# The opening of a hybrid SSD and gated-delta layer: order of the first loads, an early square-root table, and a gate tile ahead of the narrow projection

## The chip, the cores and the metric

One NeuronCore of a Trainium2 chip runs the whole program. The metric is the device time of one execution in microseconds, and a version's number is the median of three such runs.

## What is computed

One decoder layer over 1024 prompt tokens and 8 decode tokens (1032 columns in all), in float32. Only the beginning matters here: `h` is the RMS norm of the tokens, and `proj = h @ w_in` is cut into pieces, among them the narrow ones (32 step sizes `dt`, 8 `beta` and 8 `a` columns) and the merge gates (16 tiles of 128 columns).

```python
h = _rms_norm(x, norm_mix)
proj = jnp.einsum('bld,de->ble', h, w_in).astype(f32)
z, xbc, dt_raw, qkv, gate, b_raw, a_raw, mgate = _split(proj, IN_SIZES)
...
qkv, new_gdn_conv = _causal_conv(qkv, s_gdn_conv.astype(f32), gdn_conv_w.astype(f32), None)
...
dt = jax.nn.softplus(dt_raw + ssm_dt_bias.astype(f32))
...
beta = jax.nn.sigmoid(b_raw)
g = -jnp.exp(gdn_a_log.astype(f32)) * jax.nn.softplus(a_raw + gdn_dt_bias.astype(f32))
```

Behind this stand the two recurrent branches, their gated merge, a SwiGLU feed-forward, per-layer embeddings and a last norm. The change touches none of them.

## The kernel before, in words

**Dense products.** A weight tile of 1024 x 128 is loaded as one buffer `wraw` (two of them, L145 and L198) and split into a rounded part `wh` and a remainder `wl`, in two halves of four 128-row blocks each (`split_raw`, L132 to L141: the rounded part by a copy on ScalarE, L138, the remainder by a subtraction on VectorE, L139). `wh` and `wl` have three buffers each. `load_w` (L143) gives its load and its split a high priority. A product has three chunks of 344 tokens (`dense_units`, L149); a chunk takes 24 matmuls (eight blocks by three), goes into one of three PSUM banks `pd`, and is then copied out by its `evac`. Buffers and banks of one name are given out in program order.

**Who orders the work.** The tile framework has a planner: within the waits on data and buffers it arranges each engine's instructions by program order and priority, with costs of its own for every instruction. On the chip each engine then goes through its list in order. All the loads in this account are issued by SyncE's queue (SP).

**The opening (L196 to L236).** Nine token tiles `xt` (128 tokens by 1024; the ninth has 8) are asked for by SP. After the first come the five small gain loads (`gain_cols`, L114: they become columns by a transpose and a copy, L111 and L112); after the fourth come the three strided loads of the narrow columns into `wsm` (L215), which is the first `wraw` buffer and was cleared by GpSimd (L199). Then, for three parts of three tiles: a Square with a sum on ScalarE (L223), a root (L224), a reciprocal and a scaling on VectorE (L225, L226) give `xn`; per 128 channels three transposes on TensorE (L232) fill a PSUM tile (five are open at once), from which ScalarE takes the rounded `h` (L234) and VectorE the remainder (L235). A product's first chunk needs the first part alone, the second the first and second, the third the second and third.

**Behind it (L309 to L393).** The narrow product (L328) fills `x1` (48 x 1032) with ScalarE's copy-out at L326, which adds `bias`; that tile and its loads (L314, L315) lie where the opening's tiles lay. Then two gate tiles are multiplied (`fill(0, FILL[0])`, L329; `FILL[0]` is 2): `fill_units` (L290) loads a tile, multiplies it, copies it out by L296 and stores it. From the whole of `x1` a row of steps on VectorE and ScalarE computes the step sizes and their cumulative sums (L331 to L361), which are transposed into `colA`, `colB` and `colQ` (L389, L390).

**After that.** The first gated-delta head begins: `proj` (L413) multiplies a tile, copies it to `raw` (L421; two buffers), and a convolution of four steps on VectorE (L433, L435) reads `raw` and the column tile `h_g`, which is made of six loads `cst` through one buffer, with four transposes each (L407, L410, L411). The PSUM tiles of these transposes follow those of L389.

Of the kernel before, what the change touches and what calls it, by code (L numbers as in the profile page):

```python
# [8 lines left out]
F32 = mybir.dt.float32  # L9
F32R = mybir.dt.float32r  # L10
AF = mybir.ActivationFunctionType
# [5 lines left out]
P = 128  # L17
# [16 lines left out]
FILL = (2, 6, 9, 12, 15, 17, 20, 22, 24)  # L34
# [5 lines left out]
def hybrid_step(  # L40
# [9 lines left out]
    V, S, G, TE = nc.vector, nc.scalar, nc.gpsimd, nc.tensor  # L50
# [5 lines left out]
    cp = ctx.enter_context(tc.tile_pool(name="cp", bufs=1, reuse_waits="tile"))  # L56
# [36 lines left out]
    def bias_col(v, name):  # L93
        t = cp.tile([P, 1], F32, name=name)
        G.memset(t, v)
        return t

    b_eps = bias_col(EPS, "b_eps")
    b_epsq = bias_col(128.0 * EPS, "b_epsq")

    gcols = cp.tile([P, 41], F32, name="gcols")
    cwm = cp.tile([P, 120], F32, name="cwm")
# [3 lines left out]
    def gain(base, k):  # L106
        return gcols[:, base + k : base + k + 1]
# [6 lines left out]
    def gain_cols(pool):  # L114
        r0 = pool.tile([41, P], F32, name="r0")
        for src, o, n in ((norm_mix, 0, 8), (norm_ffn, 8, 8), (norm_pl, 16, 8), (ssm_norm, 24, 16), (gdn_norm, 40, 1)):
            dma(r0[o : o + n, :], src[0].rearrange("(k p) -> k p", p=P))
        to_cols(r0, gcols, 41)

    def conv_cols(pool):  # L120
        r1 = pool.tile([120, P], F32, name="r1")
        for j in range(4):
            dma(r1[24 * j : 24 * j + 24, :], ssm_conv_w[0][j].rearrange("(k p) -> k p", p=P))
        dma(r1[96:120, :], ssm_conv_b[0].rearrange("(k p) -> k p", p=P))
        r2 = pool.tile([96, P], F32, name="r2")
        for j in range(4):
            dma(r2[24 * j : 24 * j + 24, :], gdn_conv_w[0][j].rearrange("(k p) -> k p", p=P))
        to_cols(r1, cwm, 120)
        to_cols(r2, cwg, 96)


    def split_raw(raw, nk):  # L132
        parts = []
        for k0 in range(0, nk, 4):
            n = min(4, nk - k0)
            wh = wp.tile([P, 4, P], F32R, name="wh", bufs=3)
            wl = wp.tile([P, 4, P], F32R, name="wl", bufs=3)
            S.copy(wh[:, :n], raw[:, k0 : k0 + n])  # L138
            V.tensor_tensor(wl[:, :n], raw[:, k0 : k0 + n], wh[:, :n].bitcast(F32), ALU.subtract)  # L139
            parts += [(wh[:, k], wl[:, k]) for k in range(n)]  # L140
        return parts  # L141
# [7 lines left out]
    def dense_units(wt, acts, evac, chunks=CHUNKS):  # L149

        n = len(acts)
        for t0, tn in chunks:
            ps = pd.tile([P, 512], F32, name="pd")
            o = ps[:, :tn]
            for i, (ah, al) in enumerate(acts):
                wh, wl = wt[i]
                h = ah[:, t0 : t0 + tn]
                mm(o, wh, h, i == 0, False)
                mm(o, wh, al[:, t0 : t0 + tn], False, False)
                mm(o, wl, h, False, i == n - 1)  # L160
            evac(t0, tn, o)
            yield

    def dense(wt, acts, evac, chunks=CHUNKS):
        for _ in dense_units(wt, acts, evac, chunks):
            pass
# [34 lines left out]
    with (  # L201
        tc.tile_pool(name="p0", bufs=1, side="right", reuse_waits="tile") as p0,
        tc.tile_pool(name="p0x", bufs=4, side="right", reuse_waits="tile") as p0x,
    ):
        xts = []
        for tt in range(9):
            n = P if tt < 8 else NB
            xt = p0x.tile([P, D], F32, name="xt", bufs=9)
            dma(xt[:n], x_prompt[0, tt * P : tt * P + P, :] if tt < 8 else x_sample[:, 0, :])
            xts.append(xt)  # L210
            if tt == 0:
                gain_cols(p0)
            if tt == 3:
                for o, c0, m in ((0, COL_DT, 32), (R_B, COL_BETA, 8), (R_A, COL_A, 8)):
                    dma(wsm[:, :, o : o + m], w_in[:, c0 : c0 + m].rearrange("(k p) f -> p k f", p=P))  # L215
        for g in range(3):
            t0, tn = PARTS[g]
            xns = []
            for tt in range(3 * g, 3 * g + 3):
                n, xt = (P if tt < 8 else NB), xts[tt]  # L220
                xn = p0x.tile([P, D], F32, name="xn", bufs=6)
                ss = p0x.tile([P, 1], F32, name="ss", bufs=9)
                S.activation(xn[:n], xt[:n], AF.Square, accum_out=ss[:n])  # L223
                S.activation(ss[:n], ss[:n], AF.Sqrt, bias=b_eps[:n], scale=1.0 / D)  # L224
                V.reciprocal(ss[:n], ss[:n])  # L225
                V.tensor_scalar(xn[:n], xt[:n], ss[:n], None, ALU.mult)  # L226
                xns.append((xn, n))
            for k in range(KD):
                pool, name = ((pt, "pt"), (py, "py"), (pz, "pz"), (pt, "pt"), (py, "py"))[k % 5]
                t = pool.tile([P, 512], F32, name=name)  # L230
                for j, (xn, n) in enumerate(xns):
                    TE.transpose(t[:, j * P : j * P + n], xn[:n, k * P : k * P + P], ident[:n, :n])  # L232
                h, l = (a[:, t0 : t0 + tn] for a in hacts[k])
                S.activation(h, t[:, :tn], AF.Copy, scale=gain(G_MIX, k))  # L234
                V.scalar_tensor_tensor(l, t[:, :tn], gain(G_MIX, k), h.bitcast(F32), ALU.mult, ALU.subtract)  # L235
        conv_cols(p0)  # L236
# [53 lines left out]
    def fill_units(lo, hi):  # L290

        for j in range(lo, hi):
            col, dst = (COL_M + j * P, sg_d[j]) if j < 16 else (COL_G + (j - 16) * P, gate_d[j - 16])
            t = mgp.tile([P, NT], F32, name="mg")
            wt = load_w(w_in[:, col : col + P], 8)
            for i, _ in enumerate(dense_units(wt, hacts, lambda t0, tn, o: S.copy(t[:, t0 : t0 + tn], o))):  # L296
                if i == 2:
                    dma(dst, t)
                yield

    def fill(lo, hi):
        for _ in fill_units(lo, hi):
            pass
# [5 lines left out]
    with tc.tile_pool(name="pr", bufs=1, side="right", reuse_waits="tile") as pr:  # L309
# [15 lines left out]
        def ev(t0, tn, o):  # L325
            S.activation(x1[:, t0 : t0 + tn], o[:NR], AF.Identity, bias=bias)  # L326

        dense(split_raw(wsm, 8), hacts, ev)  # L328
        fill(0, FILL[0])  # L329
        beta = pr.tile([NR, NT], F32, name="beta")  # L330
        S.activation(beta[R_B : R_B + 8], x1[R_B : R_B + 8], AF.Sigmoid)  # L331
        ta = pr.tile([NR, NT], F32, name="ta")
# [1007 lines left out]
```

## Time and profile before

| | us |
|---|---|
| median of 3 runs (lowest, highest) | 2725.28 (2723.42, 2728.84) |
| the profiled execution, its own time | 2733.16 |
| its span, first to last instruction | 2731.4 |
| granted TensorE clock, mean | 0.985 |

The profiled execution is 7.9 us (0.3%) longer than the median, and 1.8 us of its time lie outside its span. TensorE is the engine that is busy nearly throughout, so the table is read with one question: in which stretches does it have nothing to do, or run at the lower clock, and what ended each of them.

### The profile page before, as it was taken

The numbers are of one execution on the slowest core, as the hardware profiler recorded it, in microseconds if no ns is written. First come the engines' busy times: TensorE is split into PE (matmuls) and PEld (weight loads), VectorE is DVE, ScalarE is ACT, GpSimd is POOL, SyncE is SP. The second block draws the span as 40 slices with busy tenths as digits, with TensorE's granted clock in tenths as the row PEclk, the third lists the DMA queues.
The fourth block names the chain that finished last, engine by engine and source line by source line (L and its number), as shares of the span: only waits on it lengthen the run. The fifth ranks groups of instructions, "written<-read, shape, count | busy, mean of one in ns | idle before, by whom it ended". The sixth has DMA issues, their size and how long they took to land.

```text
span 2731.4 us, 43746 instructions
## 1 busy us (share of the span) xinstructions
PE 2635.8 (96%) x17431; PEld 2552.8 (93%) x17431; DVE 1554.0 (57%) x2757; ACT 1013.5 (37%) x2070; POOL 241.0 (9%) x493
## 2 busy tenths in 40 slices
PE   7999999689999999999999999999999999999998
PEld 7999989689989989898999989999999999999998
DVE  6677895866657567564455566534343333333465
ACT  5455644256346364343332235422212121212243
POOL 0101120030020120110010000011000000000020
PEclk9999999899999999999999999999999999999999
DMA  3345443365355363458674347411111111111132
GB/s 122 120 149 176 143 154 102 97 135 142 102 113 152 94 149 108 106 147 228 188 216 139 114 142 257 153 48 41 47 48 44 52 42 53 41 54 40 47 88 93
DMA packets 456665, 306.34 MB, mean 112 GB/s; under 512 B 44049, under 2 KB 430010, under 8 KB 455438
## 3 DMA queue, kind: packets, MB, share of 16 engines
q1 hardware_dynamic: 454062, 295.13, 37.5%
q10 hardware_dynamic: 2400, 8.42, 0.8%
q8 instruction: 137, 2.24, 0.3%
q14 instruction: 66, 0.54, 0.1%
HBM read 227.17 MB, written 76.31 MB: 111 GB/s over the span
## 4 chain that ended last, share of the span: by engine, by line
PE 81%; DMA 6%; DVE 5%; ACT 3%; issue 2%; POOL 1%; SPq 0%; DVEq 0%; POOLq 0%; ACTq 0%
PE pd L69 72%; PE py L69 4%; DMA ab<-acum_d 2%; PE pt L69 2%; PE pz L69 1%; DMA out_dram<-so 1%; ACT ab L694 1%; DVE stmp L567 1%; DVE ca L435 1%; POOL Xt L746 1%; DVE wl L139 0%; DMA wraw<-in_w_pl_gate_dram 0%; ACT wh L138 0%; DMA mg<-y_d 0%; DMA xt<-in_x_prompt_dram 0%
## 5 line engine op out<-in xcount | busy, mean ns | idle before, releaser
L69 PE MATMUL pd<-h,wh 128*128 128x344 f32 x6384 | 1543.6, 324 | 13.8 <-ACT zt L455 9.0
L69 PEld LDWEIGHTS pd<-h,wh 128*128 128x128 f32 x6384 | 1109.9, 189 | 24.9 <-ACT zt L455 9.9
L69 PE MATMUL pd<-h,wl 128*128 128x344 f32 x3192 | 1031.2, 323 | 0.5
L69 PEld LDWEIGHTS pd<-h,wl 128*128 128x128 f32 x3192 | 604.2, 189 | 4.2 <-DVE wl L139 2.4
L138 ACT CAST wh<-wraw 128x512 fp32r<-128x512 f32 (+1 forms) x386 | 234.5, 610 | 844.7 <-PE pd L69 826.3
L139 DVE TENSOR_TENSOR wl<-wraw,wh 128x512 fp32r<-128x512 f32 (+1 forms) x386 | 263.5, 684 | 328.1 <-ACT wh L138 324.5
L69 PE MATMUL pd<-gu,wh 128*128 128x344 f32 (+2 forms) x1056 | 249.1, 320 | 0.0
L69 PE MATMUL pd<-y,wh 128*128 128x344 f32 x768 | 187.5, 325 | 0.0
L69 PEld LDWEIGHTS pd<-gu,wh 128*128 128x128 f32 x1056 | 182.3, 188 | 0.1
L69 PE MATMUL pd<-gu,wl 128*128 128x344 f32 (+2 forms) x528 | 168.9, 320 | 0.0
L694 ACT ACTIVATE ab<-ab,ncolA 128x128 f32<-128x128 f32 x256 | 81.3, 391 | 147.9 <-POOL ab L690 147.6
L69 PEld LDWEIGHTS pd<-y,wh 128*128 128x128 f32 x768 | 133.4, 190 | 1.2 <-issue 0.2
L421 ACT COPY raw<-pd 128x344 f32<-128x344 f32 x144 | 63.1, 440 | 180.6 <-PE pd L69 172.5
L69 PE MATMUL pd<-y,wl 128*128 128x344 f32 x384 | 125.4, 327 | 0.0
L1229 DVE TENSOR_TENSOR acc<-acc,pd 128x344 f32<-128x344 f32 x120 | 61.3, 512 | 103.9 <-PE pd L69 103.5
L1208 DVE TENSOR_TENSOR lt<-rb,pd 128x344 f32<-128x344 f32 x66 | 33.9, 513 | 141.4 <-PE pd L69 141.4
L1164 POOL TENSOR_TENSOR sqs<-sqs,sqt 128x1032 f32<-128x1032 f32 x12 | 30.5, 2539 | 924.1 <-ACT sqt L1163 924.1
L69 PEld LDWEIGHTS pd<-gu,wl 128*128 128x128 f32 x528 | 99.2, 188 | 0.0
L69 PE MATMUL pd<-h,gw 128*128 128x384 f32 (+1 forms) x576 | 95.9, 326 | 1.8 <-DVE pg L1259 1.8
L435 DVE SCALAR_TENSOR_TENSOR ca<-raw,cwg,ca 128x1056 f32<-128x1056 f32 x72 | 96.3, 1338 | 0.8
L435 DVE SCALAR_TENSOR_TENSOR ca<-raw,cwm,ca 128x1056 f32<-128x1056 f32 x72 | 94.6, 1315 | 1.8
L69 PEld LDWEIGHTS pd<-h,gw 128*128 128x128 f32 x576 | 92.7, 191 | 2.8 <-DVE pg L1259 2.2
(389 smaller groups left out, 3448.0 us busy)
## 6 DMA issues: line engine op xcount, KB each, us to landing
wraw<-in_w_in_dram SPq DMA_DIRECT2D x88, 512.0 KB
wraw<-in_w_ffn_in_dram SPq DMA_DIRECT2D x44, 512.0 KB
ab<-acum_d SPq DMA_DIRECT2D x32, 512.0 KB
out_dram<-sd SPq DMA_DIRECT2D x48, 256.0 KB
wraw<-in_w_ffn_out_dram SPq DMA_DIRECT2D x40, 256.0 KB
sg_d<-mg SPq DMA_DIRECT2D x16, 516.0 KB
bb<-rk_d SPq DMA_DIRECT2D x8, 1024.0 KB
sd<-in_state_ssm_dram SPq DMA_DIRECT2D x32, 256.0 KB
```

The source lines that it names most:

```text
L69: TE.matmul(o, l, r, start=start, stop=stop)
L138: S.copy(wh[:, :n], raw[:, k0 : k0 + n])
L139: V.tensor_tensor(wl[:, :n], raw[:, k0 : k0 + n], wh[:, :n].bitcast(F32), ALU.subtract)
L421: S.copy(raw[:, 3 + t0 : 3 + t0 + n], o[:, :n])
L435: V.scalar_tensor_tensor(ca, raw[:, j : j + CONVN], w[j], ca, ALU.mult, ALU.add)
L567: V.tensor_tensor(tmp[:, :i, :i], xs[:, :i, :i], bc(blk[:, :i, i], 1, [P, i, i]), ALU.mult)
L694: S.activation(ab[:, h], ab[:, h], AF.Exp, bias=ncolA[:, c, h0 + h : h0 + h + 1])
L746: G.tensor_tensor(X[i][:, cs], X[i][:, cs], eb[:, i], ALU.add)
L1164: G.tensor_tensor(sqs[:, ts], sqs[:, ts], sq[:, :tn], ALU.add)
L1208: V.tensor_tensor(dst[:, t0 : t0 + tn], rb[:, t0 : t0 + tn], o, ALU.mult)
L1229: V.tensor_tensor(a, a, o, ALU.add)
```

## The change

Four edits. A one-column activation with a square root is issued as soon as its bias column is there. The gain loads come after the third token tile and not after the first. The narrow columns' loads come after the ninth token tile and not after the fourth. The first of the two gate tiles is multiplied ahead of the narrow product.

```diff
@@ -97,6 +97,8 @@
     b_eps = bias_col(EPS, "b_eps")
     b_epsq = bias_col(128.0 * EPS, "b_epsq")
+    warm = cp.tile([P, 1], F32, name="warm")
+    S.activation(warm, b_eps, AF.Sqrt)
@@ -208,9 +210,9 @@
             xts.append(xt)
-            if tt == 0:
+            if tt == 2:
                 gain_cols(p0)
-            if tt == 3:
+            if tt == 8:
                 for o, c0, m in ((0, COL_DT, 32), (R_B, COL_BETA, 8), (R_A, COL_A, 8)):
                     dma(wsm[:, :, o : o + m], w_in[:, c0 : c0 + m].rearrange("(k p) f -> p k f", p=P))
@@ -325,8 +327,9 @@
+        fill(0, 1)
         dense(split_raw(wsm, 8), hacts, ev)
-        fill(0, FILL[0])
+        fill(1, FILL[0])
         beta = pr.tile([NR, NT], F32, name="beta")
```

## Rows read from the trace of the kernel before

**Rows 1.** The page: busy time of each engine, share of the span, instructions.

```profile
PE 2635.8 (96%) x17431; PEld 2552.8 (93%) x17431; DVE 1554.0 (57%) x2757; ACT 1013.5 (37%) x2070; POOL 241.0 (9%) x493
```

**Rows 2.** Stretches: length, busy time by engine, granted clock, DMA share, GB/s.

```profile
0.00:5.00 5.00, 0.00 (x0) 0.00 (x0) 1.42 (x3) 1.99 (x2) 2.00 (x14) 1.00 0.51 169
5.00:10.00 5.00, 0.30 (x1) 0.18 (x1) 0.39 (x3) 3.43 (x8) 0.00 (x0) 1.00 0.92 310
10.00:15.00 5.00, 3.74 (x17) 3.20 (x18) 3.33 (x7) 3.87 (x9) 0.00 (x0) 1.00 1.02 228
15.00:20.00 5.00, 3.20 (x14) 2.10 (x13) 5.00 (x11) 5.00 (x12) 0.00 (x0) 0.79 0.75 287
20.00:25.00 5.00, 5.00 (x23) 4.87 (x22) 3.46 (x8) 3.75 (x10) 0.13 (x2) 0.53 0.46 125
...
40.00:45.00 5.00, 4.01 (x25) 3.74 (x24) 2.06 (x3) 4.79 (x8) 0.00 (x0) 1.00 0.38 105
```

**Rows 3.** Timeline of SP's queue: start, duration, line, target and source.

```profile
0.82 0.39 SPq L209 DMA_DIRECT2D xt<-in_x_prompt_dram  x1
...
3.00 1.62 SPq L209 DMA_DIRECT2D xt<-in_x_prompt_dram  x3
4.66 0.43 SPq L146 DMA_DIRECT2D wraw<-in_w_in_dram  x1
5.21 6.17 SPq L215 DMA_DIRECT2D wraw<-in_w_in_dram  x3
11.43 2.01 SPq L209 DMA_DIRECT2D xt<-in_x_prompt_dram  x4
```

**Rows 4.** Timeline of ScalarE, with the idle time before and its releaser.

```profile
4.30 1.06 ACT L223 ACTIVATE xn<-xt 128x1024 f32<-128x1024 f32 x1 [2.20 <-DMA xt<-in_x_prompt_dram]
...
6.99 1.06 ACT L223 ACTIVATE xn<-xt 128x1024 f32<-128x1024 f32 x1 [1.54 <-DMA xt<-in_x_prompt_dram]
7.95 0.19 ACT L223 ACTIVATION_READ_ACCUMULATOR xn<-xt 128x1 f32 x1
8.15 1.28 ACT L224 ACT_TABLE_LOAD   x1
...
11.00 0.29 ACT L224 ACTIVATE ss<-ss,b_eps 128x1 f32<-128x1 f32 x1
...
13.44 0.58 ACT L234 ACTIVATE h<-pt,gcols 128x384 fp32r<-128x384 f32 x1 [1.10 <-PE pt L232]
...
17.35 0.66 ACT L138 CAST wh<-wraw 128x512 fp32r<-128x512 f32 x1
```

**Rows 5.** Timeline of VectorE and TensorE around the first dense matmul.

```profile
11.70 0.75 DVE L226 TENSOR_SCALAR xn<-xt,ss 128x1024 f32<-128x1024 f32 x1
...
18.06 0.94 PE L69 MATMUL pd<-h,wh 128*128 128x344 f32 x2 [1.74 <-ACT wh L138]
```

**Rows 6.** The chain that ended last: start, us, what.

```profile
11.26 0.21 PE py L232
...
24.89 0.11 PE pz L232
...
41.27 34.33 PE pd L69 x216
```

**Rows 7.** Timelines of VectorE and ScalarE from the narrow result to the first convolution.

```profile
43.63 1.23 DVE L335 SCALAR_TENSOR_TENSOR ta<-x 48x1032 f32<-48x1032 f32 x1 [0.29 <-ACT x L326]
...
92.46 0.79 DVE L433 TENSOR_SCALAR ca<-raw,cwg 128x1056 f32<-128x1056 f32 x1 [0.34 <-POOL raw L417]
...
95.12 2.67 DVE L435 SCALAR_TENSOR_TENSOR ca<-raw,cwg,ca 128x1056 f32<-128x1056 f32 x2
...
100.81 0.44 ACT L421 COPY raw<-pd 128x344 f32<-128x344 f32 x1
```

**Rows 8.** TensorE's dense matmuls alone in one stretch, and its timeline there.

```profile
93.15:106.45 13.30, 11.61 (x71) 10.78 (x70) 0.00 (x0) 1.40 (x4) 1.00 0.46 149
...
106.50 0.48 PE L69 MATMUL pd<-h,wh 128*128 128x344 f32 x2
```

## The prediction

> **What bounds the kernel now.** I read the busy times first. TensorE is busy for 96% of the span [rows 1], so a change pays where TensorE has nothing to do, or runs at the lower clock, and where nothing behind takes the gain back. The stretches [rows 2] show where that is in the opening: TensorE is idle for 5.0, 4.7, 1.3 and 1.8 us in the first four stretches of 5 us, and for 1.0 us in the stretch from 40 to 45. From 15 to 25 the granted clock is 0.79 and 0.53 of 2.4 GHz, which is the level of 1.2 GHz for part of the time; the lost share is (0.21 + 0.47) x 5 = 3.4 us. TensorE had been idle for 1.74 us just before its first dense matmul at 18.06 [rows 5].
>
> What ended that idle time is in the queue and on ScalarE. SP asks for the first token tile at 0.82 and for the next three only from 3.00, behind the five gain loads; then come the first gate tile's weights (4.66) and the three narrow loads, which hold the queue for 6.17 us, so that the fifth token tile is asked for at 11.43 [rows 3]. ScalarE waits 2.20 us for the first tile and 1.54 us for the second, and loads a second function table (1.28 us) between the second Square and the first root [rows 4]. The first `h` is written at 13.44.
>
> Next I looked behind the opening for what waits on the narrow product. `x1` is whole when L335 begins, at 43.63; VectorE's chain for the step sizes follows, and the first convolution can begin only at 92.46, runs until 97.79 and so frees its `raw` buffer; the copy-out of the third projection's first chunk, which writes that buffer, ends at 101.25 [rows 7]. That projection fills all three PSUM banks. TensorE went through 71 recorded dense matmuls, one projection of 72, from 93.15 to 106.45, and began the next one, which needs the first bank again, at 106.50 [rows 8]. So this bank is free 5.25 us before it is wanted.
>
> **The change, part by part.** The sum is made against the profiled execution (2733.16 us, of which 2731.4 are span); a difference found there is taken off the median of 2725.28. A measurement of this kernel can tell about 0.2%, 5.5 us, from no change.
>
> *Token tiles first.* Three tiles back to back, then the gains, the fourth tile and, as I read the queue, the gate weights again in tenth place. In the stretch from 5 to 10 the transfers moved 310 GB/s at a busy share of 0.92 [rows 2]; at 310/0.92 = 337 GB/s a tile of 512 KB takes 1.6 us. With the first at 4.3 as before, the others land at about 5.9, 7.5 and 9.1 and the gate weights at 10.7. The third Square, at 9.84 before, begins at 7.5 and takes 1.15 us with its read (as the second, 6.99 to 8.14 [rows 4]); before, the third tile's root began at 11.00 and its scaled tile was ready at 12.45 [rows 4, 5], so now at 10.2, and the first `h` could be written at about 10.7 or 11.1. The gain loads, five issues that move behind two tiles, land at about 6, under the Squares; if they came after 10.7 each 1 us would cost 1 us of the first `h`.
>
> *Table at once.* The load of 1.28 us goes away between the Squares; an activation of one column comes in before the first tile has landed, where ScalarE waits 2.20 us anyway [rows 4]. If that cover were gone it would cost one load and one root, 1.6 us. Most of the 1.28 us lies under the wait for the second and third tile; I count nothing beside the times above. The Trainium skill, "ScalarE: Activation LUTs", section "What ACT_TABLE_LOAD costs", adds a drain to each switch, about 2.66 us in all. The trace does not agree: the root starts right behind the 1.28 us. By the page's figure the opening would give 1.4 us more, as an estimate.
>
> *Gate tile in front.* Its weights have the highest priority and are there at 10.7; ScalarE's two casts (0.66 each [rows 4]) then stand before the eight copies of `h`, which start at 12.0 and not at 10.7. The first dense matmul follows the first `h` (0.58) at 12.6, against 18.06 [rows 5], 5.4 us earlier. Less is transposed by then (18 transposes and not 24, at 0.11 us [rows 6]), 0.6 us of work that is still to be done: 4.8 us gained. Bounds: if the casts fall behind the copies of `h`, 2 us less; if ScalarE has the first `h` at 10.7 and the casts just after it, 1.3 us more.
>
> *The stall at 40 to 45 goes.* It is the wait for the narrow copy-out, whose bias is loaded late; now a gate tile's chunks come first and are copied out without a bias: 1.0 us gained, 0 at worst.
>
> *Between the parts.* One chunk of the gate tile, one half of the narrow product's and the transposes are all that TensorE can do until the second part's `h` is there. I take 1.0 us lost, with bounds 0 and 3. The lower clock I take to cost as much as before, 3.4 us, with bounds 0 and 5.
>
> *Narrow loads last.* Their 6.17 us of issues no longer stand before five token tiles. Behind them in the queue are now only the second gate tile's weights and the convolution columns, which wait for buffers anyway. The narrow weights, at about 20 us, are covered by the gate tile's first chunk and the transposes; if that cover fails the loss is in the 1.0 above.
>
> So the gate tile and the narrow product, which end at 41.27 + 72 x 34.33/216 = 52.7 now [rows 6], end at 52.7 - (4.8 + 1.0 - 1.0) = 47.9. **That is 4.8 us gained at this point** (bounds -1 and 10).
>
> *What is late next.* The narrow product now ends last of the two. With its copy-out (some 0.5 us) and the start of L335, `x1` is whole at 48.6 and not at 43.63: 5.0 us later. Everything on the path to the first convolution hangs on it, VectorE's chain, the transposes and, behind them, the `cst` loads. The bank that was free at 101.25 is free at 106.25, or 105.65 where the copy-out, which then has ScalarE to itself, comes 0.6 sooner. TensorE, 4.8 us ahead, wants it at 101.7, and waits 4.0 us; it can do nothing else, since all three banks are held. It goes on at 105.65 instead of 106.50. The sum of both shifts is fixed: each microsecond more in the opening makes the narrow result less late, and the net gain is the opening's gain less 4.0 (bounds 3 and 5.5). **Net: 0.8 us.** 2733.16 becomes 2732.4, and the median 2724.5.
>
> **The rivals.** *The opening's gain is kept.* If the narrow product's chunks are done before the gate tile's last one, or the chain behind `x1` has more room than I find, the bank is never late. For it: in the stretch from 40 to 45 VectorE is busy for 2.06 of 5 us [rows 2]. Against it: the second half of the narrow weights needs a `wh` buffer which the gate tile gives back only in its last chunk, and the 5.25 us of room are less than the two shifts together (9.8). It gives 4.8 to 10 us, with 7 as the middle: 2718. Chance 0.25.
>
> *ScalarE stands behind the gate weights.* Its list is fixed beforehand. If the planner puts the two casts ahead of the third Square, ScalarE waits at that place until the weights land. This decides when they land after 7.5, and I expect 10.7. The Square is then at 12.0, the first `h` at some 15.2 and the first dense matmul at 15.8; the later parts move as well, the opening gains 2.3 us less the starving of up to 3, about -1, and with the 4.0 to 5.5 of the late narrow result the kernel loses 5 to 6.5: 2731. For it: the casts have the highest priority; against it: the weights follow the fourth tile in the queue. Chance 0.15.
>
> *The lower clock stays away.* The clock fell after TensorE had stood idle and came back only while dense matmuls ran [rows 2, 5]. If dense work follows the first transposes closely enough the 3.4 us are saved, and the net gain is 4.2: 2721. If the gaps between transposes are longer, as three tiles that land one by one may make them, up to 1.6 us more are lost. Chance 0.08. The Trainium skill, "TensorE: Matmul & The Clock Gate", section "What's actually happening", has the lower level as the default and the higher as what sustained work releases; the trace agrees with the order, and by that rule the earlier dense work would bring the clock back earlier.
>
> *The change does not do what it says*, since the first gate tile's weights were asked for early before as well and the rest is moved about under TensorE's later work. That is within the forecast's own range.
>
> **How the numbers follow.** The forecast, a gain in the opening that the late narrow result takes back, has 0.52, with a range of its own from 2720 to 2729 (the bounds of its terms, rarely all at one end). Kept gain 0.25, ScalarE's wait 0.15, clock 0.08. The range goes from 2716, the middle of the kept gain and some more, to 2731: about 0.1 is left out on each side. Faster by over 0.2% is below 2719.8: most of the kept gain and a little of the others, 0.27. Slower by over 0.2% is above 2730.7: 0.14, from ScalarE's wait and the tail of the forecast. The rest, 0.59, is within.
>
> **What would show it.** In the changed profile the third Square should begin near 7.5 with no table load before the roots, the casts of the gate tile near 10.7 and the first dense matmul near 12.6; both products should be done near 48. L335 should start near 48.6, and TensorE should show an idle time of some 4 us just before 106, released by a copy-out to `raw`. If that wait is not there, the kept gain is right and I am wrong by its size; if ScalarE waits for weights ahead of the third Square, the slower rival holds.

## The result, and the profile after

| | before | after |
|---|---|---|
| median, us (lowest, highest; six runs each) | 2724.76 (2722.35, 2729.67) | 2739.03 (2733.98, 2744.08) |
| profiled execution, its own time | 2733.16 | 2739.25 |
| its span | 2731.4 | 2737.5 |
| granted TensorE clock, mean | 0.985 | 0.986 |

The ratio of the means of these runs is 1.0048 (95% interval 1.0033 to 1.0063): the change makes the kernel 0.48% slower. The medians lie 14.3 us apart, and "the 14 us" below are these. The busy time of TensorE is the same as before [rows 1]:

```profile
PE 2634.1 (96%) x17431; PEld 2550.6 (93%) x17431; DVE 1552.4 (57%) x2757; ACT 1013.1 (37%) x2071; POOL 245.7 (9%) x493
```

As a ruler I use the start of the n-th recorded matmul into a `pd` bank, counted from 0 (14192 are recorded in either kernel). The 264th begins 1.8 us earlier in the changed kernel, the 384th 0.3 us earlier, the 432nd 5.0 us later and the 456th 8.6 us later (119.4 and 110.8). So the opening gained a little, and between 95 and 120 us much more was lost. The stretches show where (length; busy time and number of instructions of TensorE, its weight loads, VectorE, ScalarE and GpSimd; granted clock, DMA share, GB/s); they answer to [rows 2]:

```profile
10.00:15.00 5.00, 3.62 (x16) 3.02 (x17) 3.38 (x9) 3.14 (x9) 0.00 (x0) 1.00 0.74 284
15.00:20.00 5.00, 5.00 (x28) 4.93 (x29) 4.96 (x11) 4.68 (x11) 0.00 (x0) 1.00 0.50 122
20.00:25.00 5.00, 3.56 (x24) 2.60 (x23) 3.04 (x7) 5.00 (x13) 0.13 (x2) 1.00 0.69 147
...
30.00:35.00 5.00, 4.13 (x28) 3.21 (x26) 4.09 (x11) 3.03 (x8) 0.00 (x0) 0.94 0.01 3
...
40.00:45.00 5.00, 5.00 (x33) 5.00 (x33) 0.84 (x2) 3.00 (x5) 0.00 (x0) 1.00 0.66 211
...
85.00:90.00 5.00, 5.00 (x16) 4.00 (x17) 2.28 (x6) 1.53 (x2) 0.00 (x0) 0.56 0.73 194
90.00:95.00 5.00, 5.00 (x30) 3.83 (x28) 2.43 (x7) 1.64 (x5) 0.18 (x1) 0.76 0.10 33
...
105.00:110.00 5.00, 1.38 (x11) 1.05 (x9) 4.93 (x5) 2.04 (x3) 0.13 (x1) 0.95 0.80 227
110.00:115.00 5.00, 3.23 (x16) 2.75 (x17) 2.63 (x4) 2.63 (x8) 1.62 (x4) 0.50 0.33 125
115.00:120.00 5.00, 5.00 (x30) 5.00 (x29) 4.31 (x6) 2.14 (x4) 0.24 (x2) 0.87 0.17 64
```

From 15 to 20 and from 40 to 45 TensorE is busy throughout, where it was idle for 1.80 and 0.99 us before. But it is idle for 1.44 us from 20 to 25 and for 0.87 us from 30 to 35 (0 and 0.10 us before). From 105 to 115 it is idle for 5.39 us, and before and behind that it runs in part at 1.2 GHz: idle time and lost clock, (1 - granted clock) x busy time, come to 0.1 + 3.4 us from 80 to 105 and 5.4 + 2.3 us from 105 to 130. The kernel before shows neither between 50 and 130 us; two of its stretches:

```profile
105.00:110.00 5.00, 5.00 (x34) 5.00 (x33) 3.78 (x6) 4.06 (x8) 0.73 (x3) 1.00 0.57 168
110.00:115.00 5.00, 5.00 (x33) 5.00 (x33) 4.42 (x7) 2.86 (x7) 0.20 (x1) 1.00 0.12 45
```

The granted clock of 1.00 that the first stretches show is not borne out by the matmuls: the first two dense ones, at 15.39, took 0.92 us together, about as long as the two at 18.06 before [rows 5] and twice the 0.48 us of the two at 106.50 [rows 8]; before, a transposition took 0.21 us at 11.26 and 0.11 at 24.89 [rows 6]. So in either kernel the loss to the lower clock in the opening is larger than these rows give.

The opening first. SP's queue (start, duration, line, target and source), beside [rows 3]:

```profile
4.33 0.36 SPq L211 DMA_DIRECT2D xt<-in_x_prompt_dram  x1
...
7.43 1.57 SPq L211 DMA_DIRECT2D xt<-in_x_prompt_dram  x3
16.54 0.38 SPq L148 DMA_DIRECT2D wraw<-in_w_in_dram  x1
16.96 0.58 SPq L211 DMA_DIRECT2D xt<-in_x_prompt_dram  x1
...
18.01 3.99 SPq L217 DMA_DIRECT2D wraw<-in_w_in_dram  x3
```

The weights of the second gate tile stand ahead of the last token tiles and of the narrow loads, and wait for a buffer: the queue issues nothing from 9.00 to 16.54. ScalarE, beside [rows 4]:

```profile
7.43 1.06 ACT L225 ACTIVATE xn<-xt 128x1024 f32<-128x1024 f32 x1 [0.71 <-DMA xt<-in_x_prompt_dram]
...
8.60 1.28 ACT L101 ACT_TABLE_LOAD   x1
9.90 0.20 ACT L101 ACTIVATE warm<-b_eps 128x1 f32<-128x1 f32 x1
10.01 0.65 ACT L226 ACTIVATE ss<-ss,b_eps 128x1 f32<-128x1 f32 x3
...
13.55 0.58 ACT L236 ACTIVATE h<-pt,gcols 128x384 fp32r<-128x384 f32 x1 [1.86 <-PE pt L234]
...
14.49 1.14 ACT L140 CAST wh<-wraw 128x512 fp32r<-128x512 f32 x2
```

The third Square is 2.4 us earlier than before, and the first `h` is not (13.44 before). The planner put `warm` behind the third Square, so the table load is still there, and all three roots stand behind it.

From the narrow result to the first convolution (copy-out of the last narrow chunk, start of the chain, last transposed column, first convolution, the activation that reads its result, the copy-outs of the third projection), beside [rows 7]:

```profile
51.45 0.54 ACT L328 ACTIVATE x<-pd,rbias 48x344 f32<-48x344 f32 x1
52.19 1.22 DVE L338 SCALAR_TENSOR_TENSOR ta<-x 48x1032 f32<-48x1032 f32 x1
95.24 0.36 DVE L393 COPY colQ<-pt 128x192 f32<-128x192 f32 x1 [0.56 <-PE pt L392]
104.90 0.79 DVE L436 TENSOR_SCALAR ca<-raw,cwg 128x1056 f32<-128x1056 f32 x1
110.26 1.06 ACT L439 ACTIVATE kq<-ca 128x1024 f32<-128x1024 f32 x1 [2.30 <-DVE ca L438]
...
111.45 1.12 ACT L424 COPY raw<-pd 128x344 f32<-128x344 f32 x3
```

`x1` is whole 8.6 us later than before, and the first convolution begins 12.4 us later. TensorE's own waits, beside [rows 5, 8]:

```profile
15.39 0.92 PE L69 MATMUL pd<-h,wh 128*128 128x344 f32 x2
22.39 0.33 PE L234 MATMUL pt<-ident,xn 128*128 128x128 f32 x1 [0.88 <-DVE xn L228]
110.45 0.59 PE L413 MATMUL pt<-ident,cst 24*128 24x24 f32 x4 [4.08 <-DMA cst<-in_state_gdn_conv_dram]
111.94 0.65 PE L69 MATMUL pd<-h,wh 128*128 128x344 f32 x1 [0.90 <-ACT raw L424]
113.02 0.59 PE L413 MATMUL pt<-ident,cst 24*128 24x24 f32 x4 [0.42 <-DMA cst<-in_state_gdn_conv_dram]
```

And the queue just before that wait:

```profile
95.59 0.31 SPq L410 DMA_DIRECT2D cst<-in_state_gdn_conv_dram  x1
...
104.34 0.33 SPq L525 DMA_DIRECT2D gb<-acum_d  x1
104.83 0.38 SPq L148 DMA_DIRECT2D wraw<-in_w_in_dram  x1
106.41 4.98 SPq L410 DMA_DIRECT2D cst<-in_state_gdn_conv_dram  x2
```

The six `cst` loads pass through one buffer. The first of those that wait for it is issued at 95.59 (84.98 before). The fifth can be issued only when the fourth's transposes have run, at 106.41, behind 512 KB of `gb` and 512 KB of weights, and lands 4 us later. Its transposes stand in TensorE's list among the dense matmuls, so TensorE stops for it. But this wait is not on top of the prediction's: the next dense matmul, the 432nd, needs the bank of the third projection, whose copy-out at 111.45 stands on ScalarE behind the activation at 110.26, and that waited for the first convolution. By these rows the bank would not have been free before some 111.9 us with the fifth `cst` load there in time either; no run tests that alone.

### The profile page after: what moved, and what is told of

It is laid out like the page before. It is cut to its first block, busy times and chain, and to the rows that moved or that the text cites. A ratio compares the mean times of both kernels' runs of the same rounds, so it can differ in the third digit from the quotient of the medians.

```text
span 2737.5 us, 43750 instructions
## 1 busy us (share of the span) xinstructions
PE 2634.1 (96%) x17431; PEld 2550.6 (93%) x17431; DVE 1552.4 (57%) x2757; ACT 1013.1 (37%) x2071; POOL 245.7 (9%) x493
## 4 chain that ended last, share of the span: by engine, by line
PE 77%; DVE 7%; DMA 7%; ACT 4%; issue 3%; POOL 1%; SPq 0%; DVEq 0%; POOLq 0%; ACTq 0%
PE pd L69 68%; PE py L69 4%; PE pt L69 2%; DMA ab<-acum_d 2%; DVE ca L438 1%; PE pz L69 1%; DVE stmp L570 1%; DMA out_dram<-so 1%; ACT ab L697 1%; DMA wraw<-in_w_pl_gate_dram 1%; DVE wl L141 1%; ACT wh L140 1%; DMA DB<-dd_d 1%; DVE xs L573 1%; ACT sdt L641 0%
## 5 line engine op out<-in xcount | busy, mean ns | idle before, releaser
L69 PEld LDWEIGHTS pd<-h,wh 128*128 128x128 f32 x6384 | 1111.1, 190 | 29.7 <-ACT wh L140 10.6
```

Of the source, the lines that this page charges most:

```text
L69: TE.matmul(o, l, r, start=start, stop=stop)
```

## The experiments

Three theories. **A**: what costs is the lateness of the narrow result; everything up to the first convolution (the chain on VectorE, the transposes, the `cst` loads) comes late with it, and TensorE stands. **B**: the queue; what is moved behind others in SP's queue is the cost. **C**: any new order of the planner's lists costs some us, spread over the program. Each ratio is to the kernel before, run on the same chip (medians 2726.36 to 2727.02, 27 to 29 runs), with its 95% interval.

### Which edit costs

**The gate tile alone**, on the kernel before:

```diff
+        fill(0, 1)
         dense(split_raw(wsm, 8), hacts, ev)
-        fill(0, FILL[0])
+        fill(1, FILL[0])
```

> The kernel before with one edit: the first gate tile in front of the narrow product. Theory A (the narrow result comes too late, and the first convolution with it): x1 is whole after 50, the first convolution begins after 101 instead of at 92.46, TensorE stands idle for 4 to 8 us between 103 and 116, and the kernel is 6 to 12 us slower than before. Theory B (the queue: token tiles and narrow loads held up behind weights): the queue's order of before is kept, so the kernel is within 4 us of before. Theory C (a new arrangement by the planner, with losses spread over the kernel): a loss of any size that is not there yet at 130 us.

Measured: 2734.43 us, 1.0026 (1.0013 to 1.0039). `x1` is whole at 50.55, the first convolution begins at 101.90, and TensorE waits 4.52 us at 107.90 for a `cst` load. This one edit makes the wait, with 1.6 us less of lateness than the whole change. It does not part A from B as cleanly as was meant: the queue's order was not kept, for SP issues the second gate tile's weights at 16.30, after nothing from 13.07 on, ahead of the last three token tiles.

**The narrow loads alone**, on the kernel before (`if tt == 3` becomes `if tt == 8`):

> The kernel before with one edit of the change alone: the narrow columns are asked for after the ninth token tile. Theory A (what costs is the lateness of the narrow result, however it comes about): the narrow weights now land last, the narrow product is still first, x1 is whole some 2 to 4 us later than the 43.63 us of before and the first convolution some 5 to 8 us later than 92.46; the time is 4 to 12 us above before, and TensorE's loss is made mostly before 45 us. Theory B (the queue: token tiles come sooner, which must gain): token tiles five to nine are asked for earlier, the first dense matmul comes no later than 20 us, and the time is within 3 us of before. Theory C (the planner's lists are rearranged and the loss is spread over the program): no step in the lag of TensorE before 130 us that makes up the result.

Measured: 2731.82 us, 1.0023 (1.0013 to 1.0034). `x1` is whole at 46.19, 2.6 us late, and the first convolution begins at 98.90, 6.4 us late, both as A expected. But TensorE nowhere waits for it between 50 and 130 us. The loss is 3.5 us at the 264th dense matmul and 6.7 at the 384th, with 3.3 us of lower clock between 80 and 105: so only half of it is made early, by a first dense matmul at 28.18 and not 18.06. B's forecast falls: the token tiles were asked for earlier (the last at 7.81), and the first dense matmul came later. What the queue's wait from 9.00 to 16.54 costs in the changed kernel was not tested by itself.

**The change without the gate tile** (the order of the two products as before, the other three edits kept):

> The changed kernel with one edit undone: the narrow product is in front of both gate tiles again; the early root table, the gains after three tiles and the narrow loads last stay. Theory A: x1 is whole near 44 to 47, TensorE has no idle time of over 2 us between 100 and 120, and the kernel is within 4 us of before. Theory B: the narrow loads are still last, so the product starts late and 5 to 14 us are lost as in the changed kernel. Theory C: some loss, not at 100 to 120.

Measured: 2737.73 us, 1.0043 (1.0028 to 1.0058). A had `x1` (46.69) and the missing wait between 100 and 120 us right, but not the time; the time and the late start of the product are what B expected, though not for B's reason. The queue and TensorE's wait (SP's queue, ScalarE, TensorE):

```profile
10.10 6.25 SPq L217 DMA_DIRECT2D wraw<-in_w_in_dram  x3
...
28.00 0.60 ACT L140 CAST wh<-wraw 128x512 fp32r<-128x512 f32 x1
...
28.66 0.80 PE L69 MATMUL pd<-h,wh 128*128 128x344 f32 x3 [2.58 <-ACT wh L140]
```

The narrow loads were issued by 16.35, but their cast stands at 28.00 in ScalarE's list, behind the second part's copies, and ScalarE did not wait before it. So the first dense matmul is at 28.66 and not at 18.06 [rows 5]. It is the place in the list, not the landing, that makes it late.

**The gains alone** (`if tt == 0` becomes `if tt == 2`):

> The kernel before with the gain loads after the third token tile, nothing else. Theory A: the first three tiles are asked for back to back, the third Square begins near 7.5 us and not 9.84, the first h comes 0 to 1.5 us sooner, the narrow product stays first, so x1 and everything behind it come as much sooner: 0 to 3 us faster than before. Theory C (any new order of the lists costs several us): 3 to 8 us slower than before although the opening is no worse.

Measured: 2726.69 us, 0.9998 (0.9989 to 1.0007). The third Square begins at 7.84, the first `h` at 13.78, 0.34 us later than before: the roots are again collected behind the third Square.

**The change with a table load that is really first**:

```diff
+    wsrc = cp.tile([P, 1], F32, name="wsrc")
+    V.memset(wsrc, 1.0)
+    warm = cp.tile([P, 1], F32, name="warm")
+    S.activation(warm, wsrc, AF.Sqrt)
...
-    S.activation(warm, b_eps, AF.Sqrt)
```

> The changed kernel with the one-column root fed from a column that VectorE clears as its first instruction, so that it stands first in ScalarE's list and not behind the third Square. One table load near the start of the program and none before the roots: the first root begins at the end of the third Square (8.6 us, not 10.0), the first h near 12.2 (not 13.55) and the first dense matmul near 14.0 (not 15.39). Theory A: both products and x1 come some 1.3 us sooner, the wait before the convolution stays the same size, the time is 0.5 to 3 us below the changed kernel's, about 2737, still 9 to 13 us above before. If the late table load was the reason for the loss, the time falls to 2727 or less.

Measured: 2740.62 us, 1.0045 (1.0031 to 1.0060), no faster than the changed kernel. The opening did what was expected of it (ScalarE):

```profile
0.81 1.28 ACT L75 ACT_TABLE_LOAD   x1 [0.81 <-PEq L1333]
...
8.44 0.65 ACT L229 ACTIVATE ss<-ss,b_eps 128x1 f32<-128x1 f32 x3
...
12.28 0.58 ACT L239 ACTIVATE h<-pt,gcols 128x384 fp32r<-128x384 f32 x1 [2.15 <-PE pt L237]
```

The first `h` is 1.27 us earlier than in the changed kernel, and TensorE is 3.2 us ahead of before at the 264th dense matmul. Then it waits 4.10 us for `cst` and 0.89 us for `raw`, and is 5.7 us behind at the 456th.

**Gains and a first table load, without the two other edits**:

> Only the two edits that bring the first part of h earlier: gains after the third token tile, and the table load as ScalarE's first instruction. Narrow loads and narrow product stay where they were. Theory A: the first h comes 1 to 3 us sooner than 13.44, the first dense matmul of the narrow product some 0 to 2 us sooner than 18.06 (its weights are covered), x1 0 to 2 us sooner than 43.63, no new wait behind it: 0 to 4 us faster than before. Theory C: 3 to 8 us slower than before.

Measured: 2727.00 us, 1.0001 (0.9992 to 1.0011). Here `x1` comes with the opening, at 40.76, no wait appears between 50 and 130 us, and in the profiled execution TensorE stays 2.8 to 2.9 us ahead up to the 1500th dense matmul. In the medians nothing of it is left.

The gate tile (1.0026) and the narrow loads (1.0023) make 1.0049 together, against 1.0048 for the whole. That this is more than chance is not shown. The narrow loads alone cost through a first dense matmul at 28.18, which in the whole change comes at 15.39, and the change without the gate tile costs 1.0043, though the gains and the table load by themselves are worth nothing.

### Whether the lateness is the cause

**The lateness alone**: the kernel before, with x1 held up.

```diff
+        for _ in range(14):
+            V.tensor_scalar(x1, x1, 1.0, None, ALU.mult)
         V.scalar_tensor_tensor(ta, x1, -1.0, x1, ALU.mult, ALU.max)
```

> The kernel before with fourteen such multiplications (some 9.7 us), which is about as late as the changed kernel's x1 (8.6 us later than before). Theory A: the room of 5.25 us is gone, TensorE waits some 4.5 us just before 111 us for the copy-out to raw, and more where the lower clock follows: 4 to 8 us slower than before. If the lateness of x1 does not matter: within 2 us of before.

Measured: 2735.16 us, 1.0028 (1.0016 to 1.0039). Nothing of the opening or of the order of its loads was touched, and the changed kernel's waits are there (VectorE, TensorE):

```profile
55.82 1.23 DVE L337 SCALAR_TENSOR_TENSOR ta<-x 48x1032 f32<-48x1032 f32 x1
...
106.88 0.39 PE L412 MATMUL pt<-ident,cst 24*128 24x24 f32 x4 [2.97 <-DMA cst<-in_state_gdn_conv_dram]
109.48 0.59 PE L412 MATMUL pt<-ident,cst 24*128 24x24 f32 x4 [2.20 <-DMA cst<-in_state_gdn_conv_dram]
110.85 0.94 PE L69 MATMUL pd<-h,wh 128*128 128x344 f32 x2 [0.78 <-ACT raw L423]
```

The chain begins at 55.82, 12.2 us later than before and not 9.7 (the next run shows why), and the first convolution at 103.50, 11.0 us later; in the changed kernel 8.6 us became 12.4. TensorE is idle for 6.0 us between 80 and 130, loses 2.1 us to the lower clock behind it, and is 6.9 us behind at the 456th dense matmul. A holds, with `cst` as the releaser of the first two waits and the copy-out to `raw`, which A had named, as that of the last.

The same with seven multiplications:

> The kernel before with seven multiplications of x1 by one, on VectorE, in place, ahead of the chain (some 7 x 0.69 = 4.8 us). Theory A with the room of 5.25 us: the delay is taken up by the room, no idle time of TensorE over 0.5 us between 95 and 120 us, time within 2 us of before. If there is no such room: 3 to 5 us slower.

Measured: 2731.32 us, 1.0014 (1.0002 to 1.0026): not free, where A expected it to be. But the delay was longer than was meant. The multiplications write `x1` in place, so they had to wait until ScalarE had read it for `beta` (VectorE):

```profile
44.89 5.03 DVE L336 TENSOR_SCALAR x<-x 48x1032 f32<-48x1032 f32 x7 [2.67 <-ACT beta L331]
49.95 1.23 DVE L337 SCALAR_TENSOR_TENSOR ta<-x 48x1032 f32<-48x1032 f32 x1
```

The chain begins 6.3 us later than before, more than the room of 5.25 us, so this run cannot tell whether a delay within the room is free. The first convolution came 11.7 us late (104.16). TensorE waited only 1.76 us, for `raw` at 112.60. Most of the loss, 6.8 us in this execution, is another kind (stretches):

```profile
85.00:90.00 5.00, 5.00 (x21) 4.12 (x20) 1.21 (x4) 1.54 (x3) 0.00 (x0) 0.50 0.24 60
90.00:95.00 5.00, 5.00 (x24) 4.12 (x23) 1.41 (x3) 0.62 (x1) 0.00 (x0) 0.50 0.04 10
```

TensorE is busy throughout, and the clock is at 1.2 GHz for over 10 us. This execution took 2737.12 us, 5.8 above the median of its kernel, so the fall need not be as long in the others.

**A shorter chain**: the changed kernel leaves out the reciprocal; a straight line stands in its place.

```diff
-        V.tensor_scalar(tb, ta, 2.0, None, ALU.add)
-        V.reciprocal(tb, tb)
+        V.tensor_scalar(tb, ta, -1.0 / 6.0, 0.5, ALU.mult, ALU.add)
```

> The changed kernel, leaving out the reciprocal of 48x1032 in the chain that begins with the whole x1 (6.59 us of VectorE at L338 of before); a straight line in its argument stands in its place, so the step sizes are a rough value. Theory A: the chain is 6 to 7 us shorter, the first convolution begins near 98 us and not at 104.90, TensorE's idle time of some 5 us between 105 and 115 us falls to under 1 us, and the time is 4 to 8 us below the changed kernel's 2739. If the wait at 105 to 115 us is no cause but a loss that moves on to another place, the time falls by under 2 us.

Measured: 2732.53 us, 1.0020 (1.0010 to 1.0030), where the changed kernel has 1.0048: more than half of the loss is gone. The first convolution begins at 92.85 although `x1` is whole only at 50.61, and the idle time is gone (stretches):

```profile
105.00:110.00 5.00, 5.00 (x34) 5.00 (x33) 4.12 (x6) 3.41 (x7) 1.60 (x4) 1.00 0.54 161
110.00:115.00 5.00, 5.00 (x33) 5.00 (x33) 4.88 (x7) 4.46 (x8) 0.22 (x2) 1.00 0.14 52
```

At the 456th dense matmul this kernel is 1.6 us ahead of before, where the changed kernel is 8.6 us behind.

The control, the same edit on the kernel before:

> The control for the run without the reciprocal: the kernel before, leaving out the same reciprocal of 48x1032. Theory A: in the kernel before the bank is free 5.25 us before it is wanted, so a chain shorter by 6 to 7 us brings nothing: within 2 us of before, and no idle time of TensorE between 95 and 120 us in either. If a shorter chain pays anywhere, the time falls by 4 us or more here too.

Measured: 2734.87 us, 1.0022 (1.0010 to 1.0035). A missed here: it should have been nothing. At the 456th dense matmul this kernel is 0.6 us behind, with no idle time from 80 to 130 us; its loss comes later, and I did not find what makes it. What the pair does tell: with the short chain no cost of the change is seen (2732.53 with it, 2734.87 without), unless the control's unexplained loss hides one.

**The `cst` loads out of the way**: `h_g` made ahead of the narrow product, from a pool of its own (the six loads with their transposes, otherwise as before).

```diff
+    hgp = hgs.enter_context(tc.tile_pool(name="hgp", bufs=1, reuse_waits="tile"))
+    gdnc = Branch(hgp, hist, "g", state_gdn_conv, cwg, False, o_gdnc_p, o_gdnc_s)
...
-        gdnc = Branch(g1, hist, "g", state_gdn_conv, cwg, False, o_gdnc_p, o_gdnc_s)
```

On the kernel before:

> The kernel before, with the six loads and the transposes that make h_g put ahead of the narrow product in the program (in a pool of their own), so that they no longer come behind the transposes of the step sizes. Theory A: before, the bank was free 5 us before it was wanted, so this buys nothing there: within 3 us of before, with the first convolution some 5 to 8 us earlier than 92.46. Theories B and C: nothing as well.

Measured: 2727.70 us, 1.0002 (0.9991 to 1.0013): the first convolution 5.4 us earlier, at 87.01, and nothing gained. On the changed kernel:

> The same edit in the changed kernel. Theory A: the path from x1 to the first convolution loses the h_g loads, some 8 us, so the convolution begins near 95 to 98 instead of 104.90, TensorE's idle time between 105 and 115 goes or shrinks under 2 us, and the kernel is 5 to 9 us faster than the changed one, within 4 us of before. Theory B: the edit doesn't touch the opening's queue, so the loss stays at 9 to 14 us. Theory C: no systematic gain.

Measured: 2732.55 us, 1.0017 (1.0006 to 1.0028), so more than half of the loss (1.0048) comes back, though not all but 4 us of it, as A expected. `x1` is whole only at 54.67, but the first convolution no longer hangs on it: it begins at 79.59, where A expected 95 to 98. The wait for `cst` is gone; one for `raw` is left, later (TensorE):

```profile
124.32 0.59 PE L69 MATMUL pd<-h,wh 128*128 128x344 f32 x2 [2.15 <-ACT raw L334]
```

A second buffer for `cst` would test that wait by itself; it was not tried.

### What repeats from one execution to the next

Both kernels were profiled twice more, unchanged.

> The kernel before, unchanged, for a second profiled execution. If the clock's falls belong to the order of the work, it shows again 13.9 us of idle time and some 3 us lost to the lower clock before 50 us, and nothing between 50 and 130 us. If they differ from one execution to the next, the idle time is the same within 0.5 us and the loss to the clock is another one.

> The kernel before, a third profiled execution: idle time before 50 us within 0.5 us of 13.9, none between 50 and 130 us; the loss to the lower clock before 130 us between 0 and 3.4 us if it differs from one execution to the next, 3.0 us if it doesn't.

> The changed kernel, unchanged, for a second profiled execution. Theory A: the idle time of TensorE between 105 and 115 us is there again (5.4 us, within 1 us), since it hangs on waits alone. If the clock's falls belong to the order of the work, some 3.4 us are lost at 85 to 95 us and 2.3 us behind the idle time again; if not, one of them is missing or another one is there, and the loss made before 130 us is between 5 and 12 us instead of 8.6.

> The changed kernel, a third profiled execution: idle time between 105 and 115 us within 1 us of 5.4; lower clock behind it; the fall at 85 to 95 us there in two executions of three if it differs from one to the next.

Before took 2724.06 and 2724.81 us, the changed kernel 2739.34 and 2740.83. Idle time plus clock loss, in us, summed over stretches of 5 us:

| execution | 0 to 50 | 80 to 105 | 105 to 130 | 700 to 1300 |
|---|---|---|---|---|
| before, 1st | 14.0 + 3.0 | 0 | 0 | 17.5 + 7.8 |
| before, 2nd | 13.8 + 1.6 | 0 | 0 | 19.0 + 2.5 |
| before, 3rd | 13.7 + 1.7 | 0 | 0 | 20.4 + 2.7 |
| after, 1st | 13.4 + 1.6 | 0.1 + 3.4 | 5.4 + 2.3 | 22.0 + 5.7 |
| after, 2nd | 13.9 + 1.7 | 0.1 + 3.4 | 5.3 + 2.3 | 19.5 + 6.8 |
| after, 3rd | 13.4 + 1.7 | 0.5 + 1.7 | 5.0 + 3.4 | 20.9 + 5.2 |

One stretch for each (85 to 90 us in the second and third execution of the changed kernel, then in the third of before):

```profile
85.00:90.00 5.00, 5.00 (x17) 3.81 (x17) 2.91 (x8) 1.06 (x1) 0.00 (x0) 0.63 0.65 167
```

```profile
85.00:90.00 5.00, 5.00 (x19) 4.35 (x18) 2.76 (x7) 2.37 (x4) 0.00 (x0) 0.66 0.78 205
```

```profile
85.00:90.00 5.00, 5.00 (x34) 4.75 (x34) 0.55 (x3) 1.05 (x4) 0.29 (x2) 1.00 0.47 150
```

The idle time and the lower clock between 80 and 130 us belong to the order of the work: they are in all three executions of the one kernel and in none of the other. The clock's loss before 50 us in the kernel before does not repeat (3.0, 1.6, 1.7). Against the third execution of before, the three of the changed kernel are 9.7, 10.3 and 9.0 us behind at the 456th dense matmul, and 14.4, 14.2 and 15.4 us at the 8000th. The profiled execution that the prediction was read from had lost 6.9 us more than the third by the 8000th, nearly all of it after the 6000th, which the two others did not. That is why it was so far above the median.

So 9 to 10 of the 14 us are found. What hangs on the late narrow result is the idle time and the lower clock behind it, 7.6 to 8.4 us in the three executions; the lateness alone, in the kernel before, cost 1.0028, some 8 us. The 1.7 to 3.4 us of lower clock from 80 to 105 are not tied to it: the kernel before with `h_g` made early lost 3.4 us there with `x1` whole at 42.91, and the run with fourteen multiplications lost none. The other 4 to 5 us come in steps of 1 to 2.5 us between 165 and 1260 us in two executions; in the third most of them come at once, between 1525 and 1560. The clock costs the changed kernel 5.2 to 6.8 us from 700 to 1300, against 2.5 and 2.7 in two executions of before, but 7.8 in the other; so this isn't tied to the change, and where the 4 to 5 us come from stays open. C, as a loss without a place, falls for the first part; it isn't excluded for this one or for the loss of the control without the reciprocal.

## Why the prediction was wrong

The measured 2739.03 us lies 8 us above the range, on the side that had a chance of 0.14. The mechanism was right in outline: what is late next is the narrow result, and TensorE stands for it near 106 us. Up to the 456th dense matmul the sum has TensorE 0.8 us ahead, and it is 8.6 us behind in the profiled pair. Three terms were mis-sized: the opening's gain by 3.0 us, the wait by 1.4, and the lower clock, by size the worst, by 5.7. (Together that is 0.7 us more than the difference; the rest is not traced.) For the 4 to 5 us that are lost later the sum has no term.

- **The failed step: "That is 4.8 us gained at this point."** At the 264th dense matmul the gain was 1.8 us in the profiled pair; against the third execution of before it is 0.8, 0.1 and 1.2 us in the three executions. Its terms:
  - The first dense matmul: 15.39, not 12.6. The third Square came at 7.43 (7.5 forecast), but "now at 10.2" for the third scaled tile was wrong: I moved the third tile's steps one by one, while the planner collected the three roots behind the third Square and the table load. Then the three scalings follow one another on VectorE, and the first `h` came at 13.55. In idle time from 10 to 20 us the gain is 1.7 us (3.06 to 1.38).
  - *Table at once*, counted as hidden, did not take the load away from between the Squares and the roots. With the load really first, the first `h` gained 1.27 us, the length of the load. The Trainium skill, "ScalarE: Activation LUTs", section "What ACT_TABLE_LOAD costs", would have had 2.66 us saved; this run does not bear that out.
  - The stall from 40 to 45: gone, 0.99 us, as forecast.
  - Between the parts: 2.1 us lost (1.44 + 0.87, less 0.2 of before) where I took 1.0, within the bounds of 0 to 3.
  - *Narrow loads last*: I wrote that "behind them in the queue are now only the second gate tile's weights", which wait for a buffer anyway. The order was the other way round: those weights stood in front, and the last token tiles and the narrow loads waited behind them for 7.5 us (9.00 to 16.54).
- **"`x1` is whole at 48.6"**: 52.19. Each microsecond that the opening does not gain makes the narrow result a microsecond later; that rule of the prediction held, and its input was wrong.
- **"TensorE [...] waits 4.0 us"**: 5.4 us, by the profile for `cst` (4.08 and 0.42) and for `raw` (0.90). The bank was forecast free at 105.65 and was free near 111.9. I named the `cst` loads as hanging on the path and gave them no price. A path with one buffer and a round trip for each load does not shift by the lateness of its start alone: 8.6 us at `x1` became 10.6 at the first `cst` load that waits and 12.4 at the convolution, and with seven multiplications 6.3 became 8.4 and 11.7.
- **The second failed step: "The lower clock I take to cost as much as before, 3.4 us"**, with bounds 0 and 5: in the opening the rows show 1.6 to 1.7 us, against 1.6 to 3.0 before (the 3.4 counted the idle part of the stretch too). But 5.1 to 5.7 us more were lost between 80 and 130 us, in a part of the program for which I had set nothing.
- **The rivals.** *ScalarE stands behind the gate weights* was the case on the slower side, and it did not happen: its casts came at 14.49, with the weights there. *The gain is kept* failed by the bank, as argued against it. That *the change does not do what it says* was partly so (the table load). I had it inside the forecast's own range, where it was worth more than a microsecond of the first `h`.

## What to carry to other kernels

When work is put in front of a small product, ask first what long chain begins with the small one, and follow that chain to the last buffer it fills, through every load with a single buffer; a few us of lateness there can cost more than the opening can gain. A planner's list is part of the price: look at where it puts a "first" instruction (here behind the third Square) and at what waits for a buffer in a queue ahead of the loads that were meant to come early. Read the profile of the kernel before more than once where the change is worth a few us: here single executions differ by as much as the change's parts.

## What the runs showed of the hardware that was not expected

- The clock fell to 1.2 GHz while TensorE had no idle time (and 0.1 to 0.2 us in the 5 us before): 0.50 from 85 to 95 us in the run with seven multiplications, 0.56 to 0.66 from 85 to 90 us in all three executions of the changed kernel. Just before it and as it fell, eight transposes of 48 columns, 0.26 to 0.34 us each, lay nearly all singly between dense matmuls. In the kernel before the same eight lay so too, from 75.53 on, and the clock stayed at 1.00; with `h_g` made early, on the kernel before, it fell to 0.60 from 80 to 85 us. What makes the difference isn't known.
- In the opening SP issues the ninth load only when the first has landed: the fourth token tile, the ninth issue, starts at 4.33, when the first Square starts, and the tenth and eleventh at 5.57 and 7.43, when the second and the third do. So here, with eight loads out, a tile's place in the queue alone did not set its time.
